# Column mean of an 8192 x 8192 matrix: an eight-row ring fed by four-row loads, and VectorE adds of two rows at a time

## The chip, the cores and the metric

The kernel runs on one core of a Trainium2 chip. The metric is the device time of one execution, in microseconds (us); lower is better. A profile of one execution covers a span that is 1.7 to 2.5 us shorter than that time.

PE is TensorE's matmul side, DVE is VectorE, ACT is ScalarE, POOL is GpSimd (here it only issues loads), SP is a queue processor that issues DMAs. "Landing" is the moment at which the last byte of a load is in place. "Row" means one slice of 128 rows of x, one row for each partition: 4 MB of float32 in memory, 2 MB as bf16 on the chip.

## The reference

```python
x = np.random.randn(8192, 8192).astype(np.float32)
def reference(x): return np.mean(x, axis=0)      # 8192 column means
```

268.4 MB are read, 32 KB are written, and there is one addition for each element read. It is a streaming kernel.

## The kernel before

The POOL queue loads rows and casts them from float32 to bf16 on the way. VectorE adds most rows into a float32 `total`. TensorE sums over the partitions with a matrix of ones, and also takes the last rows. ScalarE and VectorE scale the sums out of PSUM; SP and ACT store them.

```python
K = 2                                     # rows in a load
slab_pool = tile_pool(name="slab", bufs=4)      # four slabs of two rows
def load(r0, k):                                # one load: k rows, float32 -> bf16
    t = slab_pool.tile([P, K * C], BF16, name="slab", tag="slab")
    nc.gpsimd.dma_start(out=t[:, 0 : k * C],
        in_=x[r0 : r0 + k * P, :].rearrange("(p k) c -> p (k c)", k=k))
    return t

nc.sync.dma_start(out=hx, in_=x[0:P, 0:HEADW])          # first row: 1024 columns, no cast
nc.gpsimd.dma_start(out=h2, in_=x[0:P, HEADW:C])        # first row: the other 7168

for g in range(N_GROUPS):                               # 31 loads
    t = load(P + g * K * P, K)
    if g == N_GROUPS - 1: break                         # the last one goes to TensorE
    # ... (g == 0 also adds the first row)
    for k in range(K):
        nc.vector.tensor_add(out=total, in0=total, in1=t[:, k * C : (k + 1) * C])

# the last row in six pieces on the POOL queue, then on TensorE, in this order:
#   total (float32), two rows of t (bf16), the last row piece by piece, each with drain and store
# ... (cut)
```

## Time and profile before

| | before |
|---|---|
| time, median of the first 3 runs | 627.77 us |
| span of the profile | 626.3 us |
| first packet of the POOL queue | 3.50 us |
| last packet of the last load ends | 622.55 us |
| VectorE's last add ends | 611.15 us |
| VectorE busy | 523.7 us (84%) |

The two packet times are from the trace's DMA records; the rest is on the page.

From the page: the mean busy share of the DMA engines in 40 slices of the span (in tenths, 9 is 90% or more), the bytes written, and the POOL queue's packets, MB and share.

```profile
DMA  9999999999999999999999999999999999999997
GB/s 216 203 230 205 230 205 230 205 230 205 230 205 230 205 230 205 226 209 220 216 209 224 203 232 203 233 203 232 203 230 205 230 205 230 205 229 207 228 207 137
q0 software_dynamic: 5472, 133.96, 99.6%
```

DMA has no idle slice. The GB/s are bytes written, as bf16; twice as many are read. The timeline of VectorE and PE near the end (start, duration, what, in brackets the idle time before it and what ended it):

```profile
555.03 17.42 DVE L114 TENSOR_TENSOR total<-total,slab 128x8192 f32<-128x8192 f32 x2 [1.88 <-DMA slab<-in_x_dram]
574.36 17.42 DVE L114 TENSOR_TENSOR total<-total,slab 128x8192 f32<-128x8192 f32 x2 [1.91 <-DMA slab<-in_x_dram]
593.73 17.42 DVE L114 TENSOR_TENSOR total<-total,slab 128x8192 f32<-128x8192 f32 x2 [1.96 <-DMA slab<-in_x_dram]
611.21 1.94 PE L78 MATMUL acc_80<-total,ones 128*32 128x512 f32 x8 [611.21 <-DVE total L114]
```

A slab lands every 19.3 us and costs VectorE 17.4 us. It then waits 1.9 us for the next. These waits sum to 55 us, but they are slack: VectorE keeps up with the stream. The chain of work that ended last leaves VectorE's adds near the end and runs on through one piece of DMA, from 574.82 to 622.64 (two short lines between these are left out):

```profile
563.76 8.70 DVE total L114
574.82 47.82 DMA slab<-in_x_dram
```

So the kernel ends 3.7 us after the stream does, and VectorE's end at 611.15 leaves PE enough time to be ready before the last bytes land. From the list of DMA issues (size of one, median us from issue to landing):

```profile
slab<-in_x_dram POOLq DMA_DIRECT2D x31, 4096.0 KB, 59.5
hx<-in_x_dram SPq DMA_DIRECT2D x1, 512.0 KB, 3.6
```

A load takes 19.3 us but lands 59.5 us after its issue: about two other loads are queued ahead of it.

### The profile page before, as it was taken

To read this page: it belongs to the slowest core of one execution; us is meant where nothing else is said; L and a number is where in the kernel's file an instruction comes from. 1 tells how busy PE (TensorE), PEld (TensorE's weight loads), DVE (VectorE), ACT (ScalarE), POOL (GpSimd) and SP (SyncE) were. 2 spreads that over 40 slices of the span, in tenths; PEclk is the share of its full clock that TensorE was granted. 3 is DMA by queue.
4 is the path that set the end of the run, shared out by engine and by line. 5 is a ranking of instruction groups with operands and counts; after the bars stand their busy time and mean duration, and the time that the engine had idled before them with its cause. 6 is when DMAs were issued, how large, how long until landed. Compare 5 with 4: busy or idle time off the path is not lost.

```text
span 626.3 us, 436 instructions
## 1 busy us (share of the span) xinstructions
PE 10.5 (2%) x105; PEld 4.2 (1%) x105; DVE 523.7 (84%) x67; ACT 2.8 (0%) x5; POOL 20.4 (3%) x42
## 2 busy tenths in 40 slices
PE   0000000000000000000000000000000000000006
PEld 0000000000000000000000000000000000000002
DVE  0088889988889888898888988899988889888891
ACT  0000000000000000000000000000000000000000
POOL 1000000000000000000000000000000000002000
PEclk9999999999999999999999999999999999999998
DMA  9999999999999999999999999999999999999997
GB/s 216 203 230 205 230 205 230 205 230 205 230 205 230 205 230 205 226 209 220 216 209 224 203 232 203 233 203 232 203 230 205 230 205 230 205 229 207 228 207 137
DMA packets 5661, 134.55 MB, mean 215 GB/s; under 512 B 773, under 2 KB 1038, under 8 KB 1434
## 3 DMA queue, kind: packets, MB, share of 16 engines
q0 software_dynamic: 5472, 133.96, 99.6%
q1 hardware_dynamic: 182, 0.56, 0.3%
q8 instruction: 1, 0.02, 0.0%
q14 instruction: 2, 0.02, 0.0%
q10 hardware_dynamic: 4, 0.00, 0.0%
HBM read 268.44 MB, written 0.03 MB: 429 GB/s over the span
## 4 chain that ended last, share of the span: by engine, by line
DVE 78%; DMA 13%; another core or an unknown queue 8%; issue 1%; POOL 0%; DVEq 0%; PE 0%; POOLq 0%
DVE total L114 75%; DMA slab<-in_x_dram 13%; DVE total L105 1%; DVE total L109 1%; POOL slab L147 0%; DVE total L106 0%; POOL h_96 L98 0%; DVEq L114 0%; DVE res_93 L126 0%; PE acc_85 L78 0%; PE acc_86 L78 0%; POOLq L172 0%
## 5 line engine op out<-in xcount | busy, mean ns | idle before, releaser
L114 DVE TENSOR_TENSOR total<-total,slab 128x8192 f32<-128x8192 f32 x58 | 504.1, 8692 | 56.3 <-DMA slab<-in_x_dram 55.3
L105 DVE TENSOR_TENSOR total<-slab 128x8192 f32<-128x8192 bf16 x1 | 8.7, 8693 | 32.3 <-DMA slab<-in_x_dram 32.3
L89 POOL DMA_DIRECT2D slab<-in_x_dram x31 | 16.4, 532 | 535.7 <-DVE total L114 497.5
L78 PE MATMUL acc_80<-total,ones 128*32 128x512 f32 x8 | 1.9, 1062 | 611.2 <-DVE total L114 611.2
L126 DVE TENSOR_SCALAR res_87<-acc_80 128x512 f32<-128x512 f32 x1 | 0.7, 692 | 9.0 <-PE acc_81 L78 9.0
L109 DVE TENSOR_TENSOR total<-total,h_96 128x7168 f32<-128x7168 f32 x1 | 7.6, 7618 | 0.0
L78 PEld LDWEIGHTS acc_80<-total,ones 128*32 128x32 f32 x8 | 0.2, 142 | 611.2 <-DVE total L114 611.2
L147 POOL DMA_DIRECT2D slab<-in_x_dram x6 | 3.2, 552 | 18.8 <-DVE total L114 18.8
L124 ACT ACTIVATE res_88<-acc_81 128x512 f32<-128x512 f32 x1 | 0.6, 597 | 618.1 <-PE acc_81 L78 618.1
L78 PEld LDWEIGHTS <-ones_b 128*32 128x32 bf16 x63 | 2.4, 95 | 3.0 <-issue 2.4
L78 PE MATMUL acc_80<-slab,ones_b 128*32 128x512 bf16 x12 | 2.0, 386 | 0.0
L78 PE MATMUL acc_81<-slab,ones_b 128*32 128x512 bf16 x12 | 2.0, 379 | 0.0
L78 PE MATMUL acc_81<-total,ones 128*32 128x512 f32 x8 | 1.9, 1061 | 0.0
L78 PE MATMUL acc_82<-total,ones 128*32 128x512 f32 x8 | 1.8, 1013 | 0.0
L78 PE MATMUL acc_82<-slab,ones_b 128*32 128x512 bf16 x12 | 1.7, 381 | 0.0
L78 PE MATMUL acc_83<-slab,ones_b 128*32 128x256 bf16 x12 | 1.4, 275 | 0.9 <-DMA slab<-in_x_dram 0.9
L126 DVE TENSOR_SCALAR res_91<-acc_84 64x256 f32<-64x256 f32 x1 | 0.4, 416 | 1.1 <-PE acc_84 L78 1.1
L56 ACT ACT_TABLE_LOAD x1 | 1.3, 1283 | 0.7 <-PEq L172 0.7
L78 PE MATMUL acc_84<-slab,ones_b 128*32 128x256 bf16 x6 | 1.3, 274 | 0.3 <-DMA slab<-in_x_dram 0.3
L106 DVE TENSOR_TENSOR total<-total,hx 128x1024 f32<-128x1024 f32 x1 | 1.2, 1224 | 0.0
L78 PE MATMUL acc_85<-slab,ones_b 128*32 128x192 bf16 x6 | 1.2, 247 | 0.2 <-DMA slab<-in_x_dram 0.2
L52 DVE MEMSET ones<- 128x32 f32 x1 | 0.1, 85 | 0.8 <-PEq L172 0.8
(22 smaller groups left out, 7.6 us busy)
## 6 DMA issues: line engine op xcount, KB each, us to landing
slab<-in_x_dram POOLq DMA_DIRECT2D x31, 4096.0 KB, 59.5
h_96<-in_x_dram POOLq DMA_DIRECT2D x1, 1792.0 KB, 12.6
slab<-in_x_dram POOLq DMA_DIRECT2D x1, 1024.0 KB, 45.0
hx<-in_x_dram SPq DMA_DIRECT2D x1, 512.0 KB, 3.6
slab<-in_x_dram POOLq DMA_DIRECT2D x1, 512.0 KB, 47.0
slab<-in_x_dram POOLq DMA_DIRECT2D x1, 256.0 KB, 47.8
slab<-in_x_dram POOLq DMA_DIRECT2D x1, 128.0 KB, 47.9
slab<-in_x_dram POOLq DMA_DIRECT2D x1, 96.0 KB, 47.8
```

Source lines behind the costliest of these rows:

```text
L52: nc.vector.memset(ones, 1.0)
L56: nc.scalar.mul(out=warm, in_=ones, mul=inv_r)
L78: nc.tensor.matmul(out=acc[b][j * M : (j + 1) * M, 0:w], lhsT=ones_b if cast else ones, rhs=src[:, c : c + w], start=not started[b][j], st ...
L89: nc.gpsimd.dma_start(out=t[:, 0 : k * C], in_=x[r0 : r0 + k * P, :].rearrange("(p k) c -> p (k c)", k=k),)
L105: nc.vector.tensor_add(out=total, in0=t[:, 0:C], in1=t[:, C : 2 * C])
L106: nc.vector.tensor_add(out=total[:, 0:HEADW], in0=total[:, 0:HEADW], in1=hx)
L109: nc.vector.tensor_add(out=total[:, HEADW:C], in0=total[:, HEADW:C], in1=h2)
L114: nc.vector.tensor_add(out=total, in0=total, in1=t[:, k * C : (k + 1) * C])
L124: nc.scalar.mul(out=res[b][0:rows], in_=acc[b][0:rows, 0:w], mul=inv_r)
L126: nc.vector.tensor_scalar(out=res[b][0:rows], in0=acc[b][0:rows, 0:w], scalar1=inv_r, scalar2=None, op0=mybir.AluOpType.mult,)
L147: nc.gpsimd.dma_start(out=tb[:, lo:hi], in_=last[:, lo:hi])
```

## The change

The intent: fewer, larger loads; fewer, longer VectorE instructions; an earlier start of the stream. There are four parts.

1. The four slabs become a ring of eight rows. Loads of four rows fill it at first, later loads of two.
2. VectorE adds two rows with one instruction into a pair of float32 rows. The pair is folded into one row before the last two rows are added.
3. TensorE's early rows are now two loads of one row.
4. The uncast head is split over the SP and ACT queues, straight into the sum; ScalarE copies the rest of the first row.

```diff
-    K = 2
-    N_GROUPS = (R - 2 * P) // (K * P)
+    RING = 8
+    LOADS = [4] * 8 + [2] * 14 + [1] * 2
+    PE_ROWS = 2
...
+    total = sum_pool.tile([P, 2 * C], F32, tag="total")
+    ring = ring_pool.tile([P, RING * C], BF16, tag="ring")
+    half = P // 2
+    nc.sync.dma_start(out=total[0:half, 0:HEADW], in_=x[0:half, 0:HEADW])
+    nc.scalar.dma_start(out=total[half:P, 0:HEADW], in_=x[half:P, 0:HEADW])
...
+    n_dve = len(LOADS) - PE_ROWS
+    for g, k in enumerate(LOADS):
+        t = ring[:, at * C : (at + k) * C]           # load k rows into t, then
...
+        elif g < n_dve - 1:
+            for i in range(0, k, 2):
+                nc.vector.tensor_add(out=total, in0=total, in1=t[:, i * C : (i + 2) * C])
+        elif g == n_dve - 1:
+            nc.vector.tensor_add(out=lo_, in0=lo_, in1=hi_)      # the fold
+            for i in range(k):
+                nc.vector.tensor_add(out=lo_, in0=lo_, in1=row[i])
+        elif g == n_dve:
+            for b in range(len(BLOCKS)):
+                add_chunks(t, 0, C, b)
+        else:
+            late = t
```

The output blocks and the order of drains and stores also change a little (cut).

More of the change, by code (lines that the diff above doesn't have):

```diff
@@ L30 @@
     M = P // G
-    K = 2
-    N_GROUPS = (R - 2 * P) // (K * P)
+    RING = 8
+    LOADS = [4] * 8 + [2] * 14 + [1] * 2
+    assert sum(LOADS) == R // P - 2
+    PE_ROWS = 2
     HEADW = 1024
     BLOCKS = [
-        (0, 512, 4), (2048, 512, 4), (4096, 512, 4), (6144, 256, 4), (7168, 256, 2),
-        (7680, 192, 2), (8064, 128, 1),
+        (0, 512, 4), (2048, 512, 4), (4096, 512, 4), (6144, 512, 2), (7168, 384, 2),
+        (7936, 128, 2),
     ]
     const_pool = ctx.enter_context(tc.tile_pool(name="const", bufs=1))
-    head_pool = ctx.enter_context(tc.tile_pool(name="head", bufs=1))
-    slab_pool = ctx.enter_context(tc.tile_pool(name="slab", bufs=4))
+    ring_pool = ctx.enter_context(tc.tile_pool(name="ring", bufs=1))
     sum_pool = ctx.enter_context(tc.tile_pool(name="sum", bufs=1))
@@ L54 @@
     nc.vector.memset(ones_b, 1.0)
-    warm = const_pool.tile([P, M], F32, tag="warm")
-    nc.scalar.mul(out=warm, in_=ones, mul=inv_r)
-    total = sum_pool.tile([P, C], F32, tag="total")
     acc = [
@@ L63 @@
     ]
-    res = [
+    res01 = res_pool.tile([P, 2, 512], F32, tag="res01")
+    res = [res01[:, 0, :], res01[:, 1, :]] + [
         res_pool.tile([P, w], F32, name=f"res{b}", tag=f"res{b}")
         for b, (_, w, _) in enumerate(BLOCKS)
+        if b > 1
     ]
@@ L85, in add_chunks @@
             started[b][j] = True
-    def load(r0, k):
-        t = slab_pool.tile([P, K * C], BF16, name="slab", tag="slab")
+    at = RING - 1
+    head = ring[:, at * C : (at + 1) * C]
+    nc.gpsimd.dma_start(out=head[:, HEADW:C], in_=x[0:P, HEADW:C])
+    nc.scalar.copy(out=total[:, HEADW:C], in_=head[:, HEADW:C])
+    lo_, hi_ = total[:, 0:C], total[:, C : 2 * C]
+    r0, at = P, 0
+    n_dve = len(LOADS) - PE_ROWS
+    for g, k in enumerate(LOADS):
+        t = ring[:, at * C : (at + k) * C]
@@ L89, in load @@
         nc.gpsimd.dma_start(
-            out=t[:, 0 : k * C],
+            out=t,
             in_=x[r0 : r0 + k * P, :].rearrange("(p k) c -> p (k c)", k=k),
         )
-        return t
-    hx = head_pool.tile([P, HEADW], F32, tag="hx")
-    nc.sync.dma_start(out=hx, in_=x[0:P, 0:HEADW])
-    h2 = head_pool.tile([P, C - HEADW], BF16, tag="h2")
-    nc.gpsimd.dma_start(out=h2, in_=x[0:P, HEADW:C])
-    for g in range(N_GROUPS):
-        t = load(P + g * K * P, K)
-        if g == N_GROUPS - 1:
-            break
-        if g == 0:
-            nc.vector.tensor_add(out=total, in0=t[:, 0:C], in1=t[:, C : 2 * C])
-            nc.vector.tensor_add(
-                out=total[:, 0:HEADW], in0=total[:, 0:HEADW], in1=hx
-            )
-            nc.vector.tensor_add(
-                out=total[:, HEADW:C], in0=total[:, HEADW:C], in1=h2
-            )
-            continue
-        for k in range(K):
-            nc.vector.tensor_add(out=total, in0=total, in1=t[:, k * C : (k + 1) * C])
+        r0 += k * P
@@ new lines @@
+        at = (at + k) % RING
+        row = [t[:, i * C : (i + 1) * C] for i in range(k)]
+        if g == 0:
+            nc.vector.tensor_add(out=hi_, in0=row[1], in1=row[3])
+            nc.vector.tensor_add(out=lo_, in0=lo_, in1=row[0])
+            nc.vector.tensor_add(out=lo_, in0=lo_, in1=row[2])
+        elif g < n_dve - 1:
+            for i in range(0, k, 2):
+                nc.vector.tensor_add(
+                    out=total, in0=total, in1=t[:, i * C : (i + 2) * C]
+                )
+        elif g == n_dve - 1:
[7 more added lines that the diff above has]
+            late = t
@@ L117 @@
     last = x[R - P : R, :]
-    tb = slab_pool.tile([P, K * C], BF16, name="slab", tag="slab")
+    tb = ring[:, at * C : (at + 1) * C]
     def drain(b, eng):
@@ L132, in store @@
         lo, w, g = BLOCKS[b]
-        if g == 1:
-            q.dma_start(out=out[lo : lo + w], in_=res[b][0:1, :])
-        else:
-            q.dma_start(
-                out=out[lo : lo + g * w].rearrange("(j w) -> j w", j=g),
-                in_=res[b].rearrange("(j m) w -> j m w", m=M)[0:g, 0, :],
-            )
-    PIECES = ((0, 2), (2, 3), (3, 4), (4, 5), (5, 6), (6, 7))
+        q.dma_start(
+            out=out[lo : lo + g * w].rearrange("(j w) -> j w", j=g),
+            in_=res[b].rearrange("(j m) w -> j m w", m=M)[0:g, 0, :],
+        )
+    PIECES = ((0, 2), (2, 3), (3, 4), (4, 5), (5, 6))
     spans = []
@@ L148 @@
     for b in range(len(BLOCKS)):
-        add_chunks(total, 0, C, b, cast=False)
-    for k in range(K):
-        for b in range(len(BLOCKS)):
-            add_chunks(t[:, k * C : (k + 1) * C], 0, C, b)
+        add_chunks(lo_, 0, C, b, cast=False)
+    for b in range(len(BLOCKS)):
+        add_chunks(late, 0, C, b)
     for (b0, b1), (lo, hi) in zip(PIECES, spans):
@@ L155 @@
             add_chunks(tb, lo, hi, b, stop=True)
-            drain(b, "act" if b in (1, 3, 5) else "dve")
-            store(b, nc.scalar if b == 5 else nc.sync)
+            drain(b, "act" if b in (1, 3, 4) else "dve")
+            if b == 1:
+                nc.sync.dma_start(
+                    out=out[0 : 8 * 512].rearrange("(b j w) -> j b w", b=2, j=G),
+                    in_=res01.rearrange("(j m) b w -> j m b w", m=M)[:, 0, :, :],
+                )
+            elif b > 1:
+                store(b, nc.scalar if b == 4 else nc.sync)
 _INS = ['x']
```

## The prediction

> **What bounds the kernel now.** The load stream. The slices of the page show DMA at 9 tenths or more in all but the last slice; the queue table gives the casting POOL queue 99.6% of sixteen engines' span. In the chain, ordered by time, the two-row slabs release VectorE every 19.3 us: 8.39 MB read, 434 GB/s. The Trainium skill ("DMA: Bandwidth & Descriptors", section "Where 436 GB/s comes from") gives 435 GB/s as the fabric's ceiling; the trace agrees, so the middle has nothing left. VectorE needs 17.4 us of each 19.3 (two adds of 8.69) and idles 1.9 at each slab: 55 us of waits on slabs, which are slack, not loss. 268.4 MB at 434 GB/s is 618.5 us. The DMA records run from 1.8 us (hx; the POOL queue's first packet at 3.5) to 622.6; the span is 626.3, the time 627.8. Only about 3 us at the head and 3.7 us at the tail could move.
>
> **What the change does.**
> - Four-row loads: the same bytes. The built program splits each partition's row into two pieces of 16384 elements, as large as before, so packets and rate stay.
> - One add per two rows: one add is 8.692 us for 8192 elements; 1224 against 7618 ns for 1024 and 7168 elements puts some 0.16 us in fixed cost. A two-row add should take 17.2 us. 27 of them save about 4 us of VectorE, off the critical path.
> - Ring of eight rows, four-row loads: only two loads fit, so a load is issued when VectorE finishes the one before the one in flight. Estimate: 0.3 us landing to VectorE, 34.5 us for two adds, 0.3 us to wake POOL, up to 2.5 us from issue to first packet (1.23 to 3.5 in the head) = 37.6 us of the 38.65 that a load takes. About 1 us of margin: I expect no gap in DMA, but this is tight. The later two-row loads are as deeply queued as before.
> - Head: hx on two queues, and ScalarE's copy replaces two VectorE adds. Saves 0 to 0.5 us of DMA start; the adds had slack.
> - Tail: this lies on the critical path. Before, VectorE's last slab landed at 593.7, its adds ended at 611.2, the float32 matmuls took 6.1 us and the two PE rows 2.3 us; PE was ready at about 619.6, 3 us before the last landing. Now, for the same rows, the previous two-row add ends at about 591.6, then comes the fold of the pair (8.7), then two adds (17.4): 617.8, 6.6 later. Float32 matmuls (6.1 to 6.8): 624.2; the late row (1.15): 625.4; the last row: 626.5. PE is then behind the last landing by about 3 us, and all drains and stores bunch behind it: four SP issues of 0.5 to 0.6 us and the final 2.2 us give an end near 631.
>
> **Prediction.** Span near 630.5, time 632 us (0.7% slower), 80% range 626.5 to 637. Faster by over 2%: 0.01; within 2%: 0.97; slower by over 2%: 0.02.
>
> **What would show it.** Right: the last DMA landing stays near 622.5 us; two-row adds of about 17.2 us; the last VectorE add ends near 618 and the chain ends through fold, adds, float32 matmuls and stores, not through a DMA; after the last load lands, 6 to 9 us remain instead of 3.7. Wrong: the chain still ends through the last load; or slices with DMA under 9 tenths in the first half, each four-row load starting late.
>
> **What would make it wrong.** Four-row issue taking over 1 us longer than estimated (each microsecond of starvation is paid up to six times); a slower HBM rate for 128 KB of contiguous row per partition; VectorE's f32+f32 fold faster than 8.7 us; the float32 matmuls shorter in the new blocks; a head over 1 us quicker.

## The result and the profile after

The time after is 635.46 us (median of 4 runs, 635.08 to 639.33); before, on the same chip, 628.27 us (627.69 to 629.32). The ratio is 1.0126, with a 95% interval of 1.0084 to 1.0169: slower by 1.3%, which is clear of the noise. A ratio here is the mean time of one kernel's runs over that of the other's of the same rounds, so it is not quite the ratio of the medians.

| | before | after | difference |
|---|---|---|---|
| span | 626.3 | 633.3 | +7.0 |
| first packet of the POOL queue | 3.50 | 3.74 | +0.24 |
| last packet of the last load ends | 622.55 | 624.34 | +1.8 |
| VectorE's last add ends | 611.15 | 619.56 | +8.4 |
| from the last packet to the end of the span | 3.7 | 9.0 | +5.2 |

So some 1.8 us were lost in the stream and 5.2 us behind it. The same part of the page after:

```profile
DMA  9999999999999999999999999999999999999993
GB/s 215 199 232 199 232 199 232 211 219 228 203 224 207 219 211 219 211 224 207 226 205 226 209 226 217 215 217 213 224 207 226 205 230 215 217 217 213 212 212 76
q0 software_dynamic: 5344, 133.96, 98.7%
```

The last slice is at 3 tenths of DMA, where before it was at 7. The first half still reads 9 throughout, so a loss there cannot be seen in this row. VectorE and PE near the end:

```profile
576.15 17.23 DVE L118 TENSOR_TENSOR total<-total,ring 128x16384 f32<-128x16384 f32 x1 [2.10 <-DMA ring<-in_x_dram]
593.41 8.69 DVE L122 TENSOR_TENSOR total<-total 128x8192 f32<-128x8192 f32 x1
602.14 17.42 DVE L124 TENSOR_TENSOR total<-total,ring 128x8192 f32<-128x8192 f32 x2
619.61 1.94 PE L86 MATMUL acc_78<-total,ones 128*32 128x512 f32 x8 [12.09 <-DVE total L124]
```

The fold (L122) stands between the last two-row add and the two last rows. After 576.15 VectorE never waits for a load again: it is behind. PE starts on the float32 sum at 619.61, against 611.21 before, and its last matmul, the drains and the stores all come after the last load has landed. The chain that ended last passes in this last stretch through the fold, the adds and PE, and through no load:

```profile
593.41 8.70 DVE total L122
602.14 8.70 DVE total L124
610.86 8.70 DVE total L124
619.61 1.94 PE acc_78 L86 x8
```

In the stretch of four-row loads (VectorE's adds, and POOL's issue of the load after the next):

```profile
91.18 34.48 DVE L118 TENSOR_TENSOR total<-total,ring 128x16384 f32<-128x16384 f32 x2 [13.01 <-DMA ring<-in_x_dram]
125.96 0.71 POOL L105 DMA_DIRECT2D ring<-in_x_dram  x1 [46.80 <-DVE total L118]
129.81 34.48 DVE L118 TENSOR_TENSOR total<-total,ring 128x16384 f32<-128x16384 f32 x2 [4.14 <-DMA ring<-in_x_dram]
164.59 0.70 POOL L105 DMA_DIRECT2D ring<-in_x_dram  x1 [37.93 <-DVE total L118]
169.13 34.48 DVE L118 TENSOR_TENSOR total<-total,ring 128x16384 f32<-128x16384 f32 x2 [4.84 <-DMA ring<-in_x_dram]
```

The load issued at 125.96 is next in line behind the one that lands at 129.8: the lead is about 4 us. The following landings are 39.3 us apart (129.81 to 169.13) where 38.64 us is the time that a four-row load takes without disturbance. And the DMA issues:

```profile
ring<-in_x_dram POOLq DMA_DIRECT2D x8, 8192.0 KB, 43.4
ring<-in_x_dram POOLq DMA_DIRECT2D x14, 4096.0 KB, 49.6
total<-in_x_dram SPq DMA_DIRECT2D x1, 256.0 KB, 4.6
total<-in_x_dram ACTq DMA_DIRECT2D x1, 256.0 KB, 4.7
```

A four-row load lands 43.4 us after its issue and itself takes 38.6: no second load is queued behind the one in flight any more. The two halves of the head land after 4.6 and 4.7 us, not 3.6.

### The profile page after: what moved, and what is told of

Same layout as the page of the kernel before. It is cut to its first block, busy times and chain, and to the rows that moved or that the text cites. A ratio compares the mean times of both kernels' runs of the same rounds, so it can differ in the third digit from the quotient of the medians.

```text
span 633.3 us, 356 instructions
## 1 busy us (share of the span) xinstructions
PE 11.7 (2%) x90; PEld 3.9 (1%) x90; DVE 518.7 (82%) x38; ACT 8.9 (1%) x5; POOL 17.6 (3%) x34
## 4 chain that ended last, share of the span: by engine, by line
DVE 64%; DMA 20%; another core or an unknown queue 12%; issue 2%; PE 1%; ACT 0%; DVEq 0%
DVE total L118 57%; DMA ring<-in_x_dram 20%; DVE total L124 3%; DVE total L122 1%; DVE total L114 1%; DVE total L115 1%; PE acc_78 L86 0%; PE acc_80 L86 0%; PE acc_79 L86 0%; PE acc_81 L86 0%; PE acc_82 L86 0%; ACT res_84 L139 0%; ACT res_86 L139 0%; ACT res_87 L139 0%
## 5 line engine op out<-in xcount | busy, mean ns | idle before, releaser
L118 DVE TENSOR_TENSOR total<-total,ring 128x16384 f32<-128x16384 f32 x27 | 465.1, 17225 | 50.1 <-DMA ring<-in_x_dram 49.6
L113 DVE TENSOR_TENSOR total<-ring 128x8192 f32<-128x8192 bf16 x1 | 8.7, 8692 | 51.2 <-DMA ring<-in_x_dram 51.2
L105 POOL DMA_DIRECT2D ring<-in_x_dram x24 | 14.1, 589 | 540.1 <-DVE total L118 464.9
L124 DVE TENSOR_TENSOR total<-total,ring 128x8192 f32<-128x8192 f32 x2 | 17.4, 8691 | 0.1
L86 PE MATMUL acc_78<-ring,ones_b 128*32 128x512 bf16 x12 | 2.2, 457 | 605.2 <-DMA ring<-in_x_dram 605.2
L115 DVE TENSOR_TENSOR total<-total,ring 128x8192 f32<-128x8192 f32 x1 | 8.7, 8692 | 0.0
L122 DVE TENSOR_TENSOR total<-total 128x8192 f32<-128x8192 f32 x1 | 8.7, 8691 | 0.0
L114 DVE TENSOR_TENSOR total<-total,ring 128x8192 f32<-128x8192 f32 x1 | 8.7, 8683 | 0.0
L98 ACT CAST total<-ring 128x7168 f32<-128x7168 bf16 x1 | 6.2, 6164 | 10.7 <-DMA ring<-in_x_dram 10.7
L159 POOL DMA_DIRECT2D ring<-in_x_dram x5 | 2.6, 548 | 18.3 <-DVE total L118 18.3
L86 PE MATMUL acc_79<-ring,ones_b 128*32 128x512 bf16 x12 | 2.2, 466 | 0.0
L86 PE MATMUL acc_80<-ring,ones_b 128*32 128x512 bf16 x12 | 2.2, 464 | 0.0
L86 PE MATMUL acc_78<-total,ones 128*32 128x512 f32 x8 | 1.9, 1062 | 12.1 <-DVE total L124 12.1
L86 PE MATMUL acc_79<-total,ones 128*32 128x512 f32 x8 | 1.9, 1061 | 0.0
L86 PE MATMUL acc_80<-total,ones 128*32 128x512 f32 x8 | 1.9, 1061 | 0.0
L86 PE MATMUL acc_81<-ring,ones_b 128*32 128x512 bf16 x6 | 1.4, 464 | 0.0
L86 PE MATMUL acc_81<-total,ones 128*32 128x512 f32 x4 | 1.2, 686 | 0.0
## 6 DMA issues: line engine op xcount, KB each, us to landing
ring<-in_x_dram POOLq DMA_DIRECT2D x8, 8192.0 KB, 43.4
```

What stands on the lines that cost most here:

```text
L86: nc.tensor.matmul(out=acc[b][j * M : (j + 1) * M, 0:w], lhsT=ones_b if cast else ones, rhs=src[:, c : c + w], start=not started[b][j], st ...
L98: nc.scalar.copy(out=total[:, HEADW:C], in_=head[:, HEADW:C])
L105: nc.gpsimd.dma_start(out=t, in_=x[r0 : r0 + k * P, :].rearrange("(p k) c -> p (k c)", k=k),)
L113: nc.vector.tensor_add(out=hi_, in0=row[1], in1=row[3])
L114: nc.vector.tensor_add(out=lo_, in0=lo_, in1=row[0])
L115: nc.vector.tensor_add(out=lo_, in0=lo_, in1=row[2])
```

## The experiments

Theories:

- **Tail.** The fold and the two adds after it put VectorE's end behind the stream, and PE and the stores follow: about 5 us.
- **Late issue.** With two four-row loads in the ring, the next load is issued only a few us before the one in flight ends, and the stream loses time.
- Rivals: bunched drains or the new blocks delay the end; four-row loads (128 KB of contiguous bytes for each partition) are slow in themselves; the split head delays everything.

The first four ran on one chip, which gave 627.85 us for the kernel before. The next four ran together (before 628.82), and so did the last four (before 628.46). The chip differed from group to group, so across groups the ratios are the safer comparison. The lines that declare scratch tiles are left out of the cuts.

### e1: the fold one load earlier

```diff
-    PE_ROWS = 2
+    PE_ROWS = 3                     # TensorE takes the last two-row load as well
-        elif g == n_dve:
-            for b in range(len(BLOCKS)):
-                add_chunks(t, 0, C, b)
+        elif g < len(LOADS) - 1:
+            for i in range(k):
+                for b in range(len(BLOCKS)):
+                    add_chunks(row[i], 0, C, b)
```

> The changed kernel, but the last two-row load that VectorE added now goes to TensorE, so VectorE folds the pair right after the two-row add before it. Tail theory (the fold and two more adds after the last VectorE load hold up the end by about 5 us): the last load still lands near 624.3, the end follows it by about 3.8 us instead of 9.0, span near 628, time near 630. Rival (the end is late because drains and stores are bunched or the new blocks are slower): the end stays 8 to 9 us behind the last landing, time near 635.

Measured: 632.76 us (631.96 to 633.6), ratio 1.0076 (1.0064 to 1.0089). The chain ends through the load again:

```profile
575.87 0.28 issue
576.16 1.56 POOL ring L160 x3
577.71 48.37 DMA ring<-in_x_dram
626.08 0.04 issue
626.13 0.52 PE acc L86 x2
```

The end follows the last packet (626.15) by 4.24 us instead of 9.0. This is the tail theory's step, and the rival (bunching, blocks) is out, since blocks and stores are those of the changed kernel. The time was 2.8 us above what was expected, mostly because in this run the stream itself ended at 626.1 and not at 624.3. That loss is the other theory's, and it varies from run to run.

### e2: two-row loads from the second on

```diff
-    LOADS = [4] * 8 + [2] * 14 + [1] * 2
+    LOADS = [4] + [2] * 28 + [1] * 2
```

> The changed kernel with two-row loads from the second load on, same ring, same tail. Issue theory (with two four-row loads in the ring the next is issued too late; some 1.6 to 1.9 us in all): last landing near 622.7, end near 631.6, time near 633.7, 1.5 to 2 us under the changed kernel. Rival (the landing is late for another reason, such as the head on two queues): last landing stays near 624.3, time near 635.5.

Measured: 632.37 us (631.94 to 633.6), ratio 1.0076 (1.0062 to 1.0089). The last packet ends at 622.43, as in the kernel before. VectorE's waits, first for the changed kernel and then for this one (total us, times, longest):

```profile
DVE total L118 <- DMA ring<-in_x_dram: 49.6, 12, 13.0
```

```profile
DVE total L118 <- DMA ring<-in_x_dram: 47.7, 23, 2.2
```

With two-row loads each wait is at most 2.2 us and the stream keeps its rate. The gain is over 3 us, where 1.5 to 2 was expected. Of the 3.1 us between the two profiles, 1.9 are the stream's (622.43 against 624.34). The other 1.2 lie in the float32 matmuls, which took 6.0 us from first to last here and 7.2 in the changed kernel. In both they begin at half pace (four of 512 columns in 0.85 us) and go on at full pace (0.43 us), here 3.0 us after the first of them and there 5.5. Over the profiles in which these matmuls end the kernel, that moment lies 2.9 to 5.5 us after the first. No run here ties it to the loads, so by our estimate, half of that spread, over 1 us of a single tail may be chance.

### e3: both edits

No new edit.

> Both edits at once. If the two causes add and are all there is: last landing near 622.7, span near 626.5, time near 628.2, as the kernel before within 0.5 us. Rival (something else in the change costs too, for example the eight-row ring itself or two-row adds): still 1 us or more slower than the kernel before.

Measured: 628.68 us (628.55 to 628.99), ratio 1.0011 (0.9999 to 1.0024). The last packet ends at 623.00, the span at 626.96. The two edits undo almost the whole loss. Ring, pair of sums and two-row adds stay in this version, so they cost about 0.1% (at most 0.24% by the interval); and they gain nothing.

By the ratios, times 628 us: taking the tail away is worth 0.0065, or 4.1 us, with two-row loads (e2 to e3), and 3.1 to 3.5 us with four-row loads (1.0126 and 1.0131 for the changed kernel, less 1.0076). Taking the four-row loads away is worth the same two figures. The causes nearly add.

### e5: four-row loads kept, half of their rows on TensorE

```diff
             for i in range(0, k, 2):
+                if i == 2:
+                    for r in (2, 3):
+                        for b in range(len(BLOCKS)):
+                            add_chunks(row[r], 0, C, b)
+                    continue
                 nc.vector.tensor_add(
```

> The changed kernel, four-row loads kept, but in loads 1 to 7 TensorE adds rows 2 and 3, so VectorE needs 17.2 us instead of 34.5 for each and the ring's half comes free 17 us earlier. Issue theory: four-row loads follow each other every 38.65 us, last landing near 622.7, time near 633.7. Rival (a 128 KB run per partition is itself read slower): landing stays near 624.3, time near 635.5.

Measured: 633.73 us (633.35 to 633.77), ratio 1.0090 (1.0076 to 1.0103); last packet 623.35. Loads are now issued 20 us ahead, and land at an even pace:

```profile
91.43 17.23 DVE L123 TENSOR_TENSOR total<-total,ring 128x16384 f32<-128x16384 f32 x1 [12.66 <-DMA ring<-in_x_dram]
130.02 17.23 DVE L123 TENSOR_TENSOR total<-total,ring 128x16384 f32<-128x16384 f32 x1 [21.36 <-DMA ring<-in_x_dram]
168.68 17.23 DVE L123 TENSOR_TENSOR total<-total,ring 128x16384 f32<-128x16384 f32 x1 [21.43 <-DMA ring<-in_x_dram]
```

So four-row loads can run at full rate when they are issued in time. (VectorE also works less here. That is not the reason: in e2 it works as much as in the changed kernel, and the stream keeps its rate.) One load of the seven still came 0.6 us late.

### e4: a delay that was not one

```diff
+            if k == 4:
+                for _ in range(4):
+                    nc.vector.memset(scratch, 0.0)
```

> The changed kernel with four small memsets of a scratch tile on VectorE (about 2.4 us) ahead of the adds of each later four-row load. Issue theory: VectorE's time per load becomes 36.9 us, each load is issued that much later, about 1.2 us per load are lost and the last landing moves by 6 to 8 us, time near 642. Rival (four-row transfers are slow in themselves): VectorE idles 4.1 to 4.8 us before each of these loads, so 2.4 us vanish there and the time stays near 635.5.

Measured: 636.7 us (634.87 to 639.71), ratio 1.0133. This says nothing about the theories: the memsets depend on nothing, and the scheduler moved all 28 to the start of the program (1.0 to 18.8 us), before the first four-row load had landed. The run is a repetition of the changed kernel. The test was made again as e8.

### e7: the tail alone, in the kernel before

```diff
+        if g == N_GROUPS - 2:
+            nc.vector.tensor_add(out=extra, in0=total, in1=total)   # extra: bf16, not used
         for k in range(K):
             nc.vector.tensor_add(out=total, in0=total, in1=t[:, k * C : (k + 1) * C])
```

> The kernel before with one dummy float32 add of 8192 elements (8.7 us) ahead of the adds of the last slab that VectorE takes: the tail of the change alone. Tail theory: the last add ends at 611.2 + 6.8 = 618, the last load still lands at 622.6, the end moves by about 5 us, time near 633. Rival (VectorE's end has slack there): time stays near 628.

Measured: 633.92 us (633.08 to 635.06), ratio 1.0086 (1.0069 to 1.0103).

```profile
573.81 17.42 DVE L118 TENSOR_TENSOR total<-total,slab 128x8192 f32<-128x8192 f32 x2 [1.89 <-DMA slab<-in_x_dram]
591.26 8.69 DVE L116 TENSOR_TENSOR extra<-total 128x8192 bf16<-128x8192 f32 x1
599.99 17.42 DVE L118 TENSOR_TENSOR total<-total,slab 128x8192 f32<-128x8192 f32 x2
```

The last add ends at 617.41, the last packet at 622.00, the span at 631.3: 9.3 us behind the stream. One add of 8.7 us at that place makes a kernel that is otherwise the old one 5.4 us slower (0.0086 x 628). Together with e1 this shows the tail from both sides.

### e6: the split head, in the kernel before

```diff
-    nc.sync.dma_start(out=hx, in_=x[0:P, 0:HEADW])
+    nc.sync.dma_start(out=hx[0:half, :], in_=x[0:half, 0:HEADW])
+    nc.scalar.dma_start(out=hx[half:P, :], in_=x[half:P, 0:HEADW])
```

> The kernel before with its first 512 KB split by halves of the partitions over the SP and ACT queues. If the split costs what the two traces suggest: each issue takes 0.57 us instead of 0.39, hx lands some 0.4 us later and the POOL queue's first packets start 0.2 us later; time within 0.3 us of the kernel before. If it helps as intended: first packets and last landing 0.2 to 0.5 us earlier.

Measured: 628.78 us, ratio 1.0003 (0.9988 to 1.0017). The first packet of the POOL queue comes at 3.79 us instead of 3.50. The split is no gain; it delays the stream by 0.3 us, which is below what the times can show. All profiles agree: 3.74 to 3.87 us in the ten with the split, 3.31 to 3.50 in the four without.

### a1: the changed kernel again

> The changed kernel again, unedited, to have it on the chip of the three runs beside it and to see whether its one run of 639.3 us comes again. Expected: about 635.4 us, four-row loads every 38.6 to 39.3 us, the end 9 us behind the last landing; if lateness in issuing varies from run to run, now and then a run 2 to 4 us longer.

Measured: 637.5 us (635.56 to 638.55), ratio 1.0131 (1.0107 to 1.0155). Three of the four runs were above 636.6, so the 639.3 us of the first measurement was no accident: the changed kernel spreads over some 4 us. The profiled run was a long one, with its last packet at 627.63.

### e8: the delay inside the chain

```diff
             for i in range(0, k, 2):
+                if k == 4 and i == 2:
+                    nc.vector.tensor_add(out=scratch, in0=total[:, 0:2048], in1=total[:, 0:2048])
```

> The dose that the memsets failed to give (they had been moved to the start of the program): one dummy add of 2048 elements (about 2.3 us), tied to the pair, between the two adds of each later four-row load, so that each half of the ring comes free 2.3 us later. Issue theory: six or seven loads are issued 2 us instead of 4 us before the load in flight ends, the loads come 40 us apart instead of 39, last landing and time 5 to 8 us later than the changed kernel, time 641 to 645. Rival (four-row transfers are slow in themselves): VectorE still idles about 2 us per load, no change, 635 to 638.

Measured: 637.69 us (636.95 to 640.44), ratio 1.0154 (1.0134 to 1.0174). The dose was given (VectorE's idle time fell to 1.9 and 3.2 us), but the loss hardly grew:

```profile
129.59 17.22 DVE L124 TENSOR_TENSOR total<-total,ring 128x16384 f32<-128x16384 f32 x1 [1.91 <-DMA ring<-in_x_dram]
146.85 2.29 DVE L121 TENSOR_TENSOR scratch<-total 128x2048 bf16<-128x2048 f32 x1
169.57 17.23 DVE L124 TENSOR_TENSOR total<-total,ring 128x16384 f32<-128x16384 f32 x1 [3.17 <-DMA ring<-in_x_dram]
208.40 17.23 DVE L124 TENSOR_TENSOR total<-total,ring 128x16384 f32<-128x16384 f32 x1 [2.01 <-DMA ring<-in_x_dram]
```

Landings are 40.0 and 38.8 us apart in turn. The expected 5 to 8 us did not come; by the ratios it is 1.4 us against a1 and 1.8 against the first measurement, and the intervals of a1 and e8 overlap. Taken alone, the 637.69 us lie in the range that was expected of the rival (635 to 638, four-row loads slow in themselves); it is e5 and e10 that rule the rival out. My model, in which every microsecond of delay is paid in full, fell.

### e10: a quarter of the rows on TensorE

```diff
+                if i == 2:
+                    nc.vector.tensor_add(out=lo_, in0=lo_, in1=row[2])
+                    for b in range(len(BLOCKS)):
+                        add_chunks(row[3], 0, C, b)
+                    continue
```

> The changed kernel with row 3 of loads 1 to 7 on TensorE and row 2 added alone, so that VectorE needs 26 us for each and the load is issued some 13 us ahead instead of 4. Issue theory: the lead of 13 us is as good as the 22 us of the run in which TensorE took half: loads every 38.65 us, last landing about 623, time near 633.5. Rival (four-row transfers are slow whatever the lead): time as the changed kernel, 635.5 to 637.5.

Measured: 633.53 us (633.05 to 633.89), ratio 1.0079 (1.0065 to 1.0093); last packet 622.96. A lead of 12 us is as good as one of 20.

From the DMA records of these runs (counted for this table; "lead" is from a load's issue to the last packet of the load ahead of it, "excess" is the time of the seven loads after the first over 7 x 38.64 us, "long packets" are those of 32 KB that took over 2.6 us, between 52 and 330 us, against 2.43 us as the rule):

```
run                    lead, us       excess, us    long packets
e2  two-row loads      -              -             0
e5  half on TensorE    20 to 21       0.7           2
e10 quarter            12             0.6           1
e4  (as changed)       3.4 to 4.4     2.7           20
changed, 1st profile   3.4 to 4.2     2.3           28
e1  early fold         3.5 to 4.8     3.9           46
a1  changed again      3.5 to 5.2     4.2           56
e8  dose               1.2 to 2.5     4.4           56
```

(The first two of the seven leads are left out: they are 32 and 12 us in every run of this list but the two-row one. The first was issued before the ring was full, the second after three adds of one row, 26 us, and not 34.5.) The loss appears with leads of 5 us and less and all but goes away from 12 us on. It does not grow in step with the delay below that. The rate of the whole stretch from 52.5 to 327 us agrees (busy time by engine, granted clock, DMA share, GB/s); first a1, then e10:

```profile
52.50:327.00 274.50, 0.00 (x0) 0.00 (x0) 232.69 (x15) 0.00 (x0) 5.29 (x8) 1.00 1.00 214
```

```profile
52.50:327.00 274.50, 16.23 (x126) 6.84 (x125) 184.84 (x16) 0.00 (x0) 5.30 (x8) 1.00 1.01 217
```

### e9: the kernel before with two slabs

```diff
-    slab_pool = ctx.enter_context(tc.tile_pool(name="slab", bufs=4))
+    slab_pool = ctx.enter_context(tc.tile_pool(name="slab", bufs=2))
```

> The kernel before with two slabs instead of four: the time from a load's issue to its first packets by itself. A load is then issued when VectorE has done the load before the one in flight, so two loads take 19.3 + 17.4 + 0.6 us plus the start-up L. If L is about 2.4 us (POOL's issue to the first packet in the head): 19.9 us per load, span near 650 to 655. If L is about 4.4 us (what the late loads of the changed kernel suggest: 43.1 us from issue to landing less 38.65): 20.9 us per load, span near 680. If issuing late costs nothing: near 640, from the last row alone.

Measured: 677.81 us, one run. From the chain:

```profile
69.28 22.49 DMA slab<-in_x_dram
91.85 8.70 DVE total L114
100.58 8.71 DVE total L114
109.57 24.25 DMA slab<-in_x_dram
```

A load of 19.3 us lands 22.1 to 25.5 us after its issue when it is issued 1.2 to 4.7 us (2.8 in the mean) before the last packet of the load ahead of it. The 30 loads after the first take 21.02 us each, 1.7 more than before. The loop of two loads (2 x 21.02) less VectorE (17.4), two hand-overs (0.6) and the transfer (19.3) leaves about 4.7 us for each load: some 2.8 us behind the load ahead of it and 1.7 us lost. The first packet came 1.2 to 1.8 us after the issue, so the loss is not only a wait for the first packet: 179 packets between 52 and 330 us took over 2.6 us. This is the late issue by itself, in a kernel with neither ring nor four-row loads: 50 us of it.

### e11: both edits, and the head on one queue

```diff
-    nc.sync.dma_start(out=total[0:half, 0:HEADW], in_=x[0:half, 0:HEADW])
-    nc.scalar.dma_start(out=total[half:P, 0:HEADW], in_=x[half:P, 0:HEADW])
+    nc.sync.dma_start(out=total[:, 0:HEADW], in_=x[0:P, 0:HEADW])
```

> The run with both edits, and its first 512 KB on the SP queue alone as in the kernel before. If the split of the head is what is left (0.1%): first packets of the POOL queue back at 3.4 to 3.5 us and the time 0.3 to 0.5 us under the run with both edits, equal to the kernel before within 0.3 us. Otherwise it stays near 628.7 and the rest of 0.1% is open. No gain over the kernel before is expected.

Measured: 628.69 us (628.13 to 629.42), ratio 1.0004 (0.9990 to 1.0018). The first packet is back at 3.31 us and the last ends at 622.52. The time equals the kernel before. Whether the head was the 0.1% of e3 can't be told from this: both intervals contain 1.0004. No version beats the kernel before. At its 434 GB/s the 268.4 MB take 618.5 us of its 626.3 us span, so at this rate only the few us at head and end are left to gain.

## Why the prediction was right or wrong

The measured 635.46 us lies in the range of 626.5 to 637, and "within 2%" was given 0.97. The central 632 was 3.5 us too low: 1.8 us for the stream, about 1 us for the stretch after VectorE, and 0.6 because time and span differ by 2.1 us and not by 1.5. That the time lies inside the range is in part luck: a1, the same kernel on another chip, had a median of 637.5.

- **The bound: right.** With two-row loads (e2, e3) the stream ends at 622.4 to 623.0, whatever VectorE's instructions are. The prediction took the ceiling of 435 GB/s from the Trainium skill ("DMA: Bandwidth & Descriptors", section "Where 436 GB/s comes from"); the trace's 434 agrees in size. But the page states it for the ports into SBUF, where the bf16 rows need only 217 GB/s, and for loads from HBM the same section names a lower limit, about 358 GB/s, beside a measured 425. So the number fits this stream, which exceeds both; no run here shows what sets its rate.
- **A two-row add of 17.2 us, off the path: right.** It measured 17.225. The Trainium skill ("VectorE: DVE Perf Modes", section "Side-by-side: where the cycles go for N=2048 bf16") gives about 150 cycles of init and 8 of pipe fill for an instruction and divides by 0.96 GHz, which makes an estimate of 165 ns; by the difference (2 x 8.692 - 17.225) it was 159 ns here. It was saved 27 times, and as e3 shows, to no gain.
- **The tail: right in mechanism.** The fold was predicted to move VectorE's end to 617.8; it ended at 619.56. The difference is the 1.8 us by which the last load of the two-row adds landed later (its add starts at 576.15, and the same slab's at 574.36 before). From there to the end of the span took 13.7 us against the 13 in the prediction.
- **"I expect no gap in DMA": wrong, and this is the step that failed.** The estimate of 1 us of margin used "up to 2.5 us from issue to first packet", read from a head in which one load starts on an empty machine. It was not this term that broke the sum. Loads in the changed kernel were issued 3.4 to 5.2 us ahead, and in both profiles the first packet of each late load, 1.4 to 3.0 us after its issue, started before the last packet of the load ahead had ended. What failed is the assumption that such a load costs nothing: its packets ran slower at first (28 long ones in the first profile, 56 in a1), and the stretch lost 2.3 us in the first profile, 4.2 in the second. The last landing came at 624.3 and 627.6, not "near 622.5". The prediction had named this as its main risk, but had sized it at zero.
- **Head, "saves 0 to 0.5 us": wrong sign.** The first packet came 0.24 us later (0.3 in e6). The Trainium skill ("DMA: Bandwidth & Descriptors", section "Rules for kernel authors") advises against two transfers to disjoint halves of the partitions, as they share the same engines. The traces agree: in the first profile the halves landed after 4.6 and 4.7 us, the whole in one transfer after 3.6; over all profiles the ACT half took 4.7 to 5.1 (one is not recorded), the SP half 3.6 to 4.6, the whole 3.4 to 3.6.
- **"Slices with DMA under 9 tenths" as the sign of starving: a bad sign.** There was none, even though time was lost. A slice is 16 us long; an excess of 0.7 us in 39, the most in that profile, stays above 9 tenths. Besides, a packet that takes longer counts as busy. The spacing of landings shows it.

What stays open is why a late load costs what it does. The records show its first packets taking up to 4.15 us (e1) instead of 2.43, but they do not say what these waited for. That a fixed start-up time explains it is contradicted by e8: the loop leaves about 2.7 us there and about 5 in a1, by the same sum as in e9.

## What to carry to other kernels

When a stream already sets the pace, count what a change does to the depth of its queue before counting instructions saved: two large buffers of the same total size leave the next load to be issued at the last moment, and here that cost 3 to 4 us where four smaller ones cost none. Work that moves behind the last loads is paid in full as soon as it outlasts them; one add of 8.7 us in the wrong place cost 3.1 to 5.4 us, though the engine had 50 us of idle time in all. The Trainium skill ("Perfetto Trace Analysis", section "Optimization Strategy") reads a gap that repeats on the engine that should be busy as a possible sign of too few buffers: look for it in the spacing of landings, since busy shares hid it here.

## What the Trainium skill lacked or had wrong

- "DMA: Bandwidth & Descriptors" does not say how far ahead a load of the POOL queue must be issued in a running stream. Here leads of 1.2 to 5.2 us lost 2.3 to 4.4 us over seven loads of four rows, leads of 12 us and more 0.6 to 0.7; and in e9, with leads of 1.2 to 4.7 us, each load lost 1.7 us. The page's figure of about 1 us to the first byte on that path (section "Specifications") is near the 1.2 to 1.9 us from issue to first packet in e8 and e9, but it does not cover the slower packets that followed.
- The same page's rule on disjoint halves calls the split useless; here it was also later, by over 1 us for the landing of the second half (4.7 to 5.1 against 3.4 to 3.6), 0.3 us for the stream behind it, and nothing measurable in the time.
- "TensorE: Matmul & The Clock Gate" (section "Part 1: The HAM clock gate") calls an idle TensorE half-rate by default. The clock column of the profiles seems to contradict it and does not. In e10 the column says 1.00 for the stretch below, and in e5, with twice as much work for TensorE before it, 0.50. But e10's trace has no clock record before 623.1 us, and the column reads 1.00 where there is none; e5's has 14 records, the first at 96.3 us. The pace of the matmuls decides: in e10 sets of four of 512 columns follow each other every 0.42 to 0.43 us between 91 and 325 us, at a recorded 1.00, and every 0.21 us after 625 us. So the page was right, and a clock of 1.00 must be checked against the durations. The page warns that such records may be unreliable. First e5, then e10 (busy us by engine, granted clock, DMA share, GB/s):

```profile
330.00:600.00 270.00, 0.00 (x0) 0.00 (x0) 242.70 (x15) 0.00 (x0) 10.04 (x19) 0.50 1.00 216
```

```profile
330.00:600.00 270.00, 0.00 (x0) 0.00 (x0) 251.35 (x16) 0.00 (x0) 10.04 (x19) 1.00 1.00 216
```
